# Projecting two value tiles behind the two key tiles of a streaming encoder layer, on one Trainium2 core

## The chip, the core and the metric

The kernel runs on one core of a Trainium2 chip. It is one launch. The metric is the device time of the execution in microseconds (us); lower is better. Engines are named as the profile names them: PE (TensorE matmul), PEld (its weight load), DVE (VectorE), ACT (ScalarE), POOL (GpSimd) and SP (SyncE, which here only issues DMAs).

## The reference, cut to what matters

Two layers, each `x <- x + W_out[silu(gates) * concat(A, B, C, D)]`, for a prompt of 1024 positions and 8 short requests of 16 positions (1152 positions in all). All branch inputs come from one projection of `rmsnorm(x)` (D_MODEL 1024). The change lies in branch A, the RWKV-7 time mixing:

```python
prev = concat([shift_prev, za[:, :-1]])            # token shift
zs = za + rw_mu * (prev - za)
r, k, v, wd, ad = split(zs)                         # 256, 256, 256, 64, 64 wide
decay = exp(-exp(w_log(tanh(wd))));  a = sigmoid(... ad ...)
kk = normalise(k * rw_kk);  k = k * (1 + (a - 1) * rw_ka)
for t in range(T):                                  # per head of 64
    s = s * w_t + (s @ -kk_t) (kk_t * a_t)^T + v_t k_t^T
    y_t = s @ r_t
```

The other branches are latent attention (B), a spatial gating unit (C) and trailing means (D).

## The kernel before, in words

**Layout.** Activations lie with channels on the partitions. A layer's input projection is 24 tiles of 128 output channels (`F_ORDER` gives their order, and with it the order in which weights are loaded). Each tile is made in three groups of 384 positions (g = 0, 1, 2), each group by 24 matmuls of 128x384 into one of two `pj` buffers in PSUM. `project` (L245) loops over groups, then over 8 pieces of the contraction, with three products each, since float32 is split into a high and a low part (`xh`, `xl`, `wh`, `wl`); `load_weights` (L229) makes the parts of a weight, on ACT (L241) and POOL (L242). Nearly all matmuls are issued by one helper, so their line is L76. I write K1g2 for group 2 of tile K1, and so on. After a group its *sink* runs on ACT and DVE.

**The order of branch A.** WDAD (decay and a) and K0 come together, then K1, R0, R1 (receptance), V0, V1 (values), then D0, GD0 (branch D and its gate), D1 and so on:

```python
project([(l, WDAD), (l, K0)], ...)           # K0's sink starts a_elem(0, g)
shifted(K1, ..., after_k1)                   # K1's sink starts a_elem(1, g), then queues systems(g - 1)
go("a", idle(4)); go("a", systems(2)); go("a", idle(4)); go("a", solve())
receptance(0, R0); receptance(1, R1)
values(V0); values(V1)
A.dma_start(out=shift_o[l], in_=sho)
pool_in(0, D0)
go("a", recurrence())
```

**Side work.** `a_elem`, `systems`, `solve` and `recurrence` are generators in a lane "a". While a projection is written out, `tick` takes the next step of the lane, so that its instructions stand between the projection's matmuls. A build step then orders the instructions of every engine once more and allocates the rotating buffers. Each engine runs its own list strictly in its order.

- `a_elem(i, g)` (L427 to L487): decay, `a`, the normalised key and the operands `kb` and `ar` of half i and group g. A chain over ACT and DVE that begins with a square (L437), whose sum over channels is a PE matmul `st<-ea,cr`; DVE reads it at L447 and ends the chain at L487.
- `systems(g)` (L506 to 518): for each of 18 chunks of 64 positions, four small matmuls `b<-ar,kb`, a masked copy to a two-buffer tile `ns` (DVE L514) and a DMA of it to DRAM (`nd`, for the last two `nds`; ACT's queue, L515). The operands come from both halves, so chunk 0 needs K0 and K1 of group 0.
- `solve()` (L520 to 553): loads all chunks' systems back (SP, L528 and L529), inverts them on DVE by column steps, first 16 wide, then 32 wide (31 steps of L538 and L540), copies the result transposed (L550) and writes it to DRAM (`dd`, ACT's queue, L552 and L553, two each).
- `recurrence()` (L707): the chunks in the order 16, 17 (the short requests), 0, 1, ... 15. `prepare(c)` (L560) loads the inverse (`tt`; for chunk 0 on from `dd`, SP, L571) and makes what does not need the state (gm by L580, L590 to L636). `advance(c)` (L639) carries the state (L655, L662, L666 and so on). The recurrence is queued behind D0 in both programs.
- `receptance` (L489) multiplies `ar` on POOL. `values` (L495) only writes the shifted tile `m`, which `prepare` transposes and the group norm reads; nothing of `a_elem`, `systems` or `solve` reads it.
- The shift sink (L381 to 400): ACT L383 and L386, DVE L387 and L390, for group 2 also DVE L395 and L397 and ACT L399 and L400.
- GD0's sink: ACT L756 to L758, DVE L759, the matmul `st<-m,pbd`, DVE L820, a DMA (ACT's queue, L822).

Of the kernel before, what the change touches and what calls it, by code (L numbers as in the profile page):

```python
# [31 lines left out]
(WDAD, K0, R0, V0, K1, R1, V1, D0, GD0, D1, GD1, VC0, VC1, U0, GC0, U1, GC1,  # L32
 GB0, GB1, Q0, Q1K, CK, GA0, GA1) = range(NF)

F_ORDER = (WDAD, K0, K1, R0, R1, V0, V1, D0, GD0, D1, GD1, VC0, VC1, U0, GC0, U1, GC1,
           Q0, Q1K, CK, GB0, GB1, GA0, GA1)


# [10 lines left out]
def tile_trunk(ctx: ExitStack, tc: tile.TileContext, *aps):  # L49
# [37 lines left out]
    def nm(p):  # L87
        cnt[0] += 1
        return f"{p}_{cnt[0]}"
# [20 lines left out]
    def s_tile(tag, bufs, cols=G):  # L110
        return sp_.tile([128, cols], F32, tag=tag, name=nm(tag), bufs=bufs)
# [13 lines left out]
    def go(lane, gen):  # L125
        lanes.setdefault(lane, deque()).append(gen)

    def start(lane, gen):
        next(gen)
        go(lane, gen)  # L130
# [26 lines left out]
    def gcols(g):  # L157
        return slice(g * G, (g + 1) * G)
# [39 lines left out]
    def raw_weights(fi, src):  # L198

        raw[fi] = m_tile(1024).rearrange("p (k t) -> p k t", k=8)  # L200
        SY.dma_start(out=raw[fi], in_=src)
# [3 lines left out]
    SY.dma_start(out=vcs, in_=vec.rearrange("l p n -> p l n"))  # L205
    raw_weights(0, win[0, F_ORDER[0]])
    raw_weights(1, win[0, F_ORDER[1]])
    next(first[1])
# [15 lines left out]
    for l in range(L):  # L224
        plan += [((l, f), win[l, f], range(8)) for f in F_ORDER]
        plan += [((l, NF + f), wout[l, f], out_order) for f in range(8)]
# [118 lines left out]
    for l in range(L):  # L345
# [11 lines left out]
        def vcol(i):  # L357
            return vc[:, i:i + 1]

        def inproj(f, sink):  # L360
            ticks = (3,)
            if f in (K1, R0, R1, V0, V1, D0, GD0, D1, GD1, VC0, VC1, GC0, U1, GC1,
                     GA0, GA1):
                ticks = (2, 5)
            elif f in (U0, GB0, GB1):
                ticks = (1, 3, 5)
            project([(l, f)], xh, xl, [sink], ticks)
# [8 lines left out]
        def shift_sink(f, dest, after=None):  # L376
            last = {}

            def sink(g, ps):
                mu, om = vcol(V_MU + f), nv[:, f:f + 1]  # L380
                zs = dest(g)  # L381
                n = min(G, TP - g * G)
                A.activation(out=zs, in_=ps, func=AF.Copy, scale=om)  # L383
                if n == G:
                    last[g] = smp.tile([128, 1], F32, tag="lc", name=nm("lc"), bufs=4)
                    A.activation(out=last[g], in_=ps[:, G - 1:G], func=AF.Copy)  # L386
                V.scalar_tensor_tensor(out=zs[:, 1:n], in0=ps[:, 0:n - 1], scalar=mu, in1=zs[:, 1:n],  # L387
                                       op0=ALU.mult, op1=ALU.add)
                if g > 0:
                    V.scalar_tensor_tensor(out=zs[:, 0:1], in0=last[g - 1], scalar=mu, in1=zs[:, 0:1],  # L390
                                           op0=ALU.mult, op1=ALU.add)
                if n < G:
                    samp = ps[:, n:].rearrange("p (s t) -> p s t", t=SL)
                    zv = zs[:, n:].rearrange("p (s t) -> p s t", t=SL)
                    V.scalar_tensor_tensor(out=zv[:, :, 1:], in0=samp[:, :, :SL - 1], scalar=mu, in1=zv[:, :, 1:],  # L395
                                           op0=ALU.mult, op1=ALU.add)
                    V.scalar_tensor_tensor(out=zv[:, :, 0], in0=sh0[:, f, :], scalar=mu, in1=zv[:, :, 0],  # L397
                                           op0=ALU.mult, op1=ALU.add)
                    A.activation(out=sho[:, f, 0:1], in_=ps[:, n - 1:n], func=AF.Copy)  # L399
                    A.activation(out=sho[:, f, 1:], in_=samp[:, :, SL - 1], func=AF.Copy)  # L400
                if after:
                    after(g, zs)
            return sink

        def shifted(f, dest, after=None):
            inproj(f, shift_sink(f, dest, after))
# [20 lines left out]
        def a_elem(i, g, k):  # L427
            kb = abp.tile([128, 6, 2, 64], F32, tag="ab", name=nm("kb"))
            ar = abp.tile([128, 6, 2, 64], F32, tag="ab", name=nm("ar"))
            KB[i][g], AR[i][g] = kb, ar  # L430
            gc = gcols(g)

            def ea():
                return s_tile("ea", EA)

            q = ea()
            A.activation(out=q, in_=k, func=AF.Square, scale=vcol(V_KK + i))  # L437
            yield

            pw, pk, pa = st(), st(), pb()  # L440
            mm(pw[:, :G], wlo[0:64, i * 128:(i + 1) * 128], z6[0:64, gc])
            mm(pa[:, :G], wlo[64:128, i * 128:(i + 1) * 128], z6[64:128, gc])
            mm(pk[:, :G], bd1, q)
            rw, av = ea(), ea()
            A.activation(out=rw, in_=pw[:, :G], func=AF.Exp, scale=-1.0, bias=nv[:, 7 + i:8 + i])
            A.activation(out=av, in_=pa[:, :G], func=AF.Exp, scale=-1.0, bias=nv[:, 9 + i:10 + i])
            V.tensor_scalar(out=q, in0=pk[:, :G], scalar1=1e-24, scalar2=None, op0=ALU.max)  # L447
            recip1p(rw)
            cs = ea()
            n = min(G, TP - g * G)  # L450
            V.tensor_tensor_scan(out=cs, data0=smask[:, 0:G] if n == G else smask[:, 128:], data1=rw, initial=0.0,
                                 op0=ALU.mult, op1=ALU.add)
            yield
            A.activation(out=q, in_=q, func=AF.Ln)
            A.activation(out=q, in_=q, func=AF.Exp, scale=-0.5)
            ex = ar[:, :, 1, :]
            A.activation(out=ex, in_=chv(cs), func=AF.Exp, scale=-DECAY_C)
            nch = n // 64
            Po.tensor_copy(out=Pend[:, i, g * 6:g * 6 + nch], in_=ex[:, :nch, 63])
            if n < G:  # L460
                Po.tensor_copy(out=PendS[:, i, :].rearrange("p (c s) -> p c s", c=2),
                               in_=ex[:, nch:].rearrange("p c (s t) -> p c s t", t=SL)[:, :, :, SL - 1])
            V.tensor_tensor(out=rw, in0=cs, in1=rw, op=ALU.subtract)
            ep = rw
            A.activation(out=ep, in_=rw, func=AF.Exp, scale=-DECAY_C)
            ei = cs
            A.activation(out=ei, in_=cs, func=AF.Exp, scale=DECAY_C)
            yield

            kk = q  # L470
            V.scalar_tensor_tensor(out=kk, in0=k, scalar=vcol(V_KK + i), in1=q, op0=ALU.mult, op1=ALU.mult)
            V.scalar_tensor_tensor(out=ar[:, :, 0, :], in0=chv(kk), scalar=-1.0, in1=chv(ep),
                                   op0=ALU.mult, op1=ALU.mult)

            recip1p(av)
            yield
            t = ea()
            V.tensor_tensor(out=t, in0=av, in1=ei, op=ALU.mult)
            for hh in range(2):
                pr = slice(64 * hh, 64 * hh + 64)  # L480
                V.tensor_tensor(out=kb[pr, :, hh, :], in0=chv(kk)[pr], in1=chv(t)[pr], op=ALU.mult)  # L481
            V.tensor_scalar(out=av, in0=av, scalar1=vcol(V_KA + i), scalar2=nv[:, 11 + i:12 + i],
                            op0=ALU.mult, op1=ALU.add)
            V.tensor_tensor(out=av, in0=av, in1=ei, op=ALU.mult)
            for hh in range(2):
                pr = slice(64 * hh, 64 * hh + 64)
                V.tensor_tensor(out=kb[pr, :, 1 - hh, :], in0=chv(k)[pr], in1=chv(av)[pr], op=ALU.mult)  # L487

        def receptance(i, fr):  # L489
            def after(g, zs):  # L490
                ex = AR[i][g][:, :, 1, :]
                Po.tensor_tensor(out=ex, in0=chv(zs), in1=ex, op=ALU.mult)
            shifted(fr, lambda g: s_tile("gn", 3), after)

        def values(fv):  # L495
            v = m_tile()
            shifted(fv, lambda g: v[:, gcols(g)])
            vfm.append(v)
# [406 lines left out]
        def after_k1(g, zs):  # L905
            start("a", a_elem(1, g, zs))
            if g > 0:
# [2 lines left out]
        project([(l, WDAD), (l, K0)], xh, xl,  # L910
                [shift_sink(WDAD, lambda g: z6[:, gcols(g)], tanh_part),
                 shift_sink(K0, lambda g: zk0[:, gcols(g)], lambda g, zs: start("a", a_elem(0, g, zs)))])
        shifted(K1, lambda g: zk1[:, gcols(g)], after_k1)
        go("a", idle(4))
        go("a", systems(2))
        go("a", idle(4))
        go("a", solve())
        receptance(0, R0)
        receptance(1, R1)
        values(V0)  # L920
        values(V1)
        A.dma_start(out=shift_o[l], in_=sho)
        pool_in(0, D0)
        go("a", recurrence())
# [638 lines left out]
```

## Time and profile before

| what | value |
|---|---|
| runs | 1456.58, 1454.72, 1450.95 us (median 1454.72) |
| profiled execution, own time | 1454.34 us |
| its span, first to last instruction | 1452.5 us |
| PE busy | 1373.0 us, 95% |
| DVE, ACT, POOL busy | 54%, 51%, 30% |
| mean granted TensorE clock | 0.987 |

The profile is of one execution. A row of the timeline gives the start in us from the span's start, the duration, engine, line, operation, output and inputs; in brackets the idle time of the engine before it and what ended it. PE's matmuls overlap: a 128x384 row lasts 0.33 us, while in an undisturbed run the next starts after 0.17 us. A float32 matmul of the small kinds is shown as two passes (x8 for a chunk's four).

### The profile page before, as it was taken

Reading aid. Unit: us, or ns where it says so; the run is one execution under the profiler, and the core shown is the slowest. Engines: PE = TensorE matmul, PEld = TensorE weight load, DVE = VectorE, ACT = ScalarE, POOL = GpSimd, SP = SyncE. Lnnn points to the kernel's source line nnn. Section 1 sums busy time; section 2 is a strip of 40 time slices with the busy share of each in tenths; the row PEclk is TensorE's granted clock in tenths of the full one; section 3 lists DMA queues with packets and bytes.
Section 4 is the critical chain, followed back from the end, with each engine's and each line's share of the span. In section 5 each row is a group of like instructions: output and inputs, shape, how many; then the busy total and the mean of one; then the engine's idle time right before and its main releaser. Section 6 shows DMA issues by size and latency. Waiting matters only on the chain. (4 is left out here: it accounts for less than half of the span.)

```text
span 1452.5 us, 26772 instructions
## 1 busy us (share of the span) xinstructions
PE 1373.0 (95%) x9938; PEld 1154.8 (80%) x9938; DVE 783.5 (54%) x1762; ACT 740.7 (51%) x1985; POOL 437.7 (30%) x576
## 2 busy tenths in 40 slices
PE   4899889999999999999989998999999999999999
PEld 3678878888988876679977787788799788666998
DVE  6985944445236557742287858543532474767211
ACT  6772244555366667642257521555643776666210
POOL 4514414336411110322162333332652111112320
PEclk9999999999999999999989999999999999999999
DMA  7213241110312114033301123221022111131232
GB/s 221 52 34 79 56 102 49 56 45 31 103 34 77 53 35 132 3 119 98 88 22 30 50 64 71 85 71 48 31 74 66 58 57 54 44 102 44 70 98 76
DMA packets 116594, 97.38 MB, mean 67 GB/s; under 512 B 46128, under 2 KB 111344, under 8 KB 116464
## 3 DMA queue, kind: packets, MB, share of 16 engines
q1 hardware_dynamic: 76776, 73.74, 17.6%
q10 hardware_dynamic: 39688, 21.94, 5.0%
q8 instruction: 78, 1.28, 0.4%
q14 instruction: 52, 0.43, 0.1%
HBM read 71.48 MB, written 24.16 MB: 66 GB/s over the span
## 5 line engine op out<-in xcount | busy, mean ns | idle before, releaser
L76 PE MATMUL pj<-xh,wh 128*128 128x384 f32 x1152 | 413.8, 360 | 18.0 <-ACT xh L280 7.3
L76 PE MATMUL pj<-xl,wh 128*128 128x384 f32 x1152 | 395.5, 343 | 3.7 <-POOL xl L282 2.7
L76 PE MATMUL pj<-xh,wl 128*128 128x384 f32 x1152 | 395.4, 343 | 0.0
L242 POOL TENSOR_TENSOR wl<-wr,wh 128x256 fp32r<-128x256 f32 x200 | 156.2, 789 | 463.8 <-ACT wh L241 387.5
L76 PEld LDWEIGHTS pj<-xh,wh 128*128 128x128 f32 x1152 | 220.7, 192 | 40.7 <-ACT sho L400 10.0
L76 PEld LDWEIGHTS pj<-xl,wh 128*128 128x128 f32 x1152 | 221.1, 192 | 11.2 <-POOL xl L282 4.7
L76 PEld LDWEIGHTS pj<-xh,wl 128*128 128x128 f32 x1152 | 220.7, 192 | 6.1 <-issue 4.8
L76 PE MATMUL pj<-yh,wh 128*128 128x384 f32 x384 | 130.0, 339 | 2.7 <-DVE x L1386 2.7
L76 PE MATMUL pj<-yh,wl 128*128 128x384 f32 x384 | 129.2, 337 | 0.0
L76 PE MATMUL pj<-yl,wh 128*128 128x384 f32 x384 | 129.0, 336 | 0.0
L241 ACT ACTIVATE wh<-wr 128x256 fp32r<-128x256 f32 x200 | 80.9, 414 | 86.0 <-PE pj L76 41.5
L76 PEld LDWEIGHTS pj<-yh,wh 128*128 128x128 f32 x384 | 72.5, 189 | 4.0 <-DVE x L1386 3.0
L242 POOL TENSOR_TENSOR wl<-m,wh 128x256 fp32r<-128x256 f32 x56 | 43.6, 788 | 103.7 <-ACT wh L241 76.4
L76 PEld LDWEIGHTS pj<-yl,wh 128*128 128x128 f32 x384 | 72.6, 189 | 0.1
L76 PEld LDWEIGHTS pj<-yh,wl 128*128 128x128 f32 x384 | 72.6, 189 | 0.1
L1261 ACT ACTIVATE X<-b,ng 128x512 f32<-128x512 f32 (+3 forms) x96 | 55.0, 576 | 28.7 <-DVE ng L1253 25.0
L76 PEld LDWEIGHTS st<-X,X 128*64 128x64 f32 x576 | 35.5, 136 | 31.6 <-DVE mx L1249 6.3
L76 PE MATMUL b<-sp,cr 128*128 128x384 f32 (+3 forms) x192 | 59.2, 389 | 1.0 <-POOL sp L99 0.6
L1249 DVE TENSOR_REDUCE mx<-b 128x1 f32<-128x512 f32 (+3 forms) x96 | 53.0, 552 | 8.5 <-PE b L76 6.9
L1382 DVE TENSOR_TENSOR pt<-pj,pt 128x384 f32<-128x384 f32 x24 | 13.4, 557 | 80.6 <-PE pj L76 80.6
L241 ACT ACTIVATE wh<-m 128x256 fp32r<-128x256 f32 x56 | 22.5, 413 | 62.2 <-PE pj L76 61.1
L76 PE MATMUL st<-X,X 128*64 128x128 f32 x576 | 53.3, 283 | 0.3
(296 smaller groups left out, 2558.1 us busy)
## 6 DMA issues: line engine op xcount, KB each, us to landing
wr<-in_win_dram SPq DMA_DIRECT2D x176, 128.0 KB
m<-in_wout_dram SPq DMA_DIRECT2D x12, 512.0 KB
x<-in_xT_dram SPq DMA_DIRECT2D x12, 384.0 KB
ysp<-m ACTq DMA_DIRECT2D x24, 192.0 KB
pt<-in_xT_dram SPq DMA_DIRECT2D x24, 192.0 KB
ea<-ysp SPq DMA_DIRECT2D x24, 192.0 KB
x1d<-x ACTq DMA_DIRECT2D x24, 192.0 KB
pt<-x1d SPq DMA_DIRECT2D x24, 192.0 KB
```

What stands on the lines that cost most here:

```text
L76: return PE.matmul(out, lhsT=lhsT, rhs=rhs, start=start, stop=stop, skip_group_check=True)
L241: A.activation(out=h, in_=r, func=AF.Copy)
L242: Po.tensor_tensor(out=lo, in0=r, in1=h.bitcast(F32), op=ALU.subtract)
L1249: V.tensor_reduce(out=mx[:, b:b + 1], in_=pc[:, :w], axis=AX.X, op=ALU.max)
L1261: A.activation(out=P[:, :w], in_=pc[:, :w], func=AF.Exp, scale=SCALE, bias=ng, accum_out=sums[pr][:, b, s, h:h + 1])
L1382: V.tensor_tensor(out=xr, in0=ps, in1=xr, op=ALU.add)
```

## The change

The two calls of `values` move: V0 stands between K0 and K1, V1 in front of R0. `F_ORDER` follows, so the weights are loaded in that order. No operation is added or taken away, and every operand is the same.

```diff
-F_ORDER = (WDAD, K0, K1, R0, R1, V0, V1, D0, GD0, D1, GD1, VC0, VC1, U0, GC0, U1, GC1,
+F_ORDER = (WDAD, K0, V0, K1, V1, R0, R1, D0, GD0, D1, GD1, VC0, VC1, U0, GC0, U1, GC1,
...
+        values(V0)
         shifted(K1, lambda g: zk1[:, gcols(g)], after_k1)
         go("a", idle(4))
         go("a", systems(2))
         go("a", idle(4))
         go("a", solve())
+        values(V1)
         receptance(0, R0)
         receptance(1, R1)
-        values(V0)
-        values(V1)
         A.dma_start(out=shift_o[l], in_=sho)
         pool_in(0, D0)
```

Three places of the first layer show what becomes of the engines' lists; the second layer's are alike.

**PE, where key 1's first sum stands.** `st<-ea,cr` is the sum over channels that `a_elem(1, 0)` waits for. Before, behind five matmuls of K1g2 (here `pj_873`):

```order
L76 MATMUL pj_805<-xh_332,wl_635 128x384
L76 MATMUL b_960<-ar_441,kb_440 64x64 x2
L76 MATMUL pj_873<-xh_405,wh_591 128x384
L76 MATMUL pj_873<-xl_406,wh_591 128x384
L76 MATMUL pj_873<-xh_405,wl_592 128x384
L76 MATMUL pj_873<-xh_405,wh_591 128x384
L76 MATMUL pj_873<-xl_406,wh_591 128x384
L76 MATMUL st_791<-ea_780,cr 128x384
```

Now, behind twelve matmuls of K1g1 (`pj_921`):

```order
L76 MATMUL pj_921<-xh_332,wl_676 128x384
L76 MATMUL pj_921<-xh_332,wh_675 128x384
L76 MATMUL pj_921<-xl_333,wh_675 128x384
L76 MATMUL pj_921<-xh_332,wl_676 128x384
L76 MATMUL st_907<-ea_904,cr 128x384
L76 MATMUL pj_921<-xh_332,wh_695 128x384
```

Counted from K0's end, 53 projection matmuls stood ahead of it (K1g0, K1g1 and five), and now 108 (V0's 72, K1g0 and twelve). K1g2 is followed at once by the first chunks of `systems` in both.

**ACT, at the write of the inverses to `dd`** (`pt_1940` and `pt_2045` are the gates of GD0g0 and GD0g1). Before, it stands ahead of both gates:

```order
L595 ACTIVATE vu_1886<-b_1879 64x2x64 x2
L552 DMA dd_291<-m_1394 64x32x32
L553 DMA dd_291<-m_1393 64x32x32
L552 DMA dd_291<-m_1394 64x32x32
L553 DMA dd_291<-m_1393 64x32x32
L610 ACTIVATE m_1931<-b_1898 128x2x128 x2
L756 ACTIVATE pt_1940<-pj_1856 128x384
```

Now, behind both:

```order
L756 ACTIVATE pt_2045<-pj_1983 128x384
L757 ACTIVATE pt_2045<-pt_2045,eps 128x384
L758 ACTIVATE pt_2045<-pt_2045 128x384
L241 ACTIVATE wh_2090<-wr_2088 128x256
L241 ACTIVATE wh_2120<-wr_2118 128x256
L822 DMA ysp_316<-m_1662 128x384
L241 ACTIVATE wh_2132<-wr_2130 128x256
L241 ACTIVATE wh_2177<-wr_2175 128x256
L552 DMA dd_291<-m_1504 64x32x32
L553 DMA dd_291<-m_1503 64x32x32
```

GD0's first two gates, chunk 16's L610 and the four weight pieces of the group after them no longer queue behind the inverses.

**DVE, inside the 32-wide inversion.** Before, the gates' and chunk 16's operations come after the inversion's copy L550:

```order
L655 TENSOR_TENSOR u_380_1954<-b_1956,u_380_1954 128x128
L580 TENSOR_TENSOR gm_1964<-b_1965,cm 128x256
L759 TENSOR_TENSOR pt_1940<-pj_1856,pt_1940 128x384
L580 TENSOR_TENSOR gm_1964<-b_1969,cm 128x256
L820 SCALAR_TENSOR_TENSOR m_1717<-st_1945,vcs,pt_1940 128x384
L759 TENSOR_TENSOR pt_2045<-pj_1983,pt_2045 128x384
L820 SCALAR_TENSOR_TENSOR m_1717<-st_2050,vcs,pt_2045 128x384
```

Now, they stand between its steps:

```order
L540 TENSOR_TENSOR m_1504<-m_1504,m_1505 128x19x13
L655 TENSOR_TENSOR u_380_1954<-b_1956,u_380_1954 128x128
L538 TENSOR_TENSOR m_1505<-m_1504,m_1503 128x240
L759 TENSOR_TENSOR pt_1940<-pj_1856,pt_1940 128x384
L540 TENSOR_TENSOR m_1504<-m_1504,m_1505 128x20x12
L820 SCALAR_TENSOR_TENSOR m_1662<-st_1945,vcs,pt_1940 128x384
L538 TENSOR_TENSOR m_1505<-m_1504,m_1503 128x231
L580 TENSOR_TENSOR gm_1964<-b_1965,cm 128x256
```

With them an L728 and the two sinks of R1's last groups stand between the inversions' steps now, and the sinks of V0g2 and V1, which stood there, come before them.

In PE's list the tail differs too: from chunk 0's product with `tt` to D1g2's first matmul stood 57 projection matmuls (the last nine of GD0g2, D1g0 and D1g1) and one `st<-m,pbd`; now 21 projection matmuls (of D1g1). From D1g2 on the lists of both programs hold the same operations in the same order: PE's third group of D1 is preceded by the same part of chunk 1.

## Rows read from the trace of the kernel before

**Rows 1.** Windows: start and end, length, then for each engine (PE, PEld, DVE, ACT, POOL) its busy time and, in brackets, its instructions, then the granted TensorE clock as a share of full speed, the busy share of the DMA engines, and GB/s. In order: layer 1 (of two) from K1 to D1g2; the chains of a_elem(1, 0) and (1, 1); the inversions; from chunk 0's product with `tt` to D1g2; an undisturbed stretch of PE; a stretch behind a wait of PE.

```profile
67.70:223.77 156.07, 142.46 (x1100) 123.21 (x1099) 109.10 (x258) 63.34 (x182) 50.01 (x71) 0.98 0.26 66
80.00:100.00 20.00, 17.89 (x106) 12.92 (x104) 19.07 (x38) 15.04 (x38) 4.74 (x8) 1.00 0.08 27
141.17:185.77 44.60, 39.25 (x274) 36.82 (x273) 41.91 (x118) 9.60 (x28) 17.11 (x25) 0.97 0.23 56
201.78:223.77 21.99, 21.75 (x270) 18.50 (x266) 9.19 (x20) 10.55 (x40) 7.29 (x11) 1.00 0.28 88
710.00:720.00 10.00, 10.00 (x59) 10.00 (x58) 2.55 (x5) 1.89 (x4) 2.07 (x3) 1.00 0.33 98
182.60:186.40 3.80, 3.58 (x17) 3.35 (x18) 2.93 (x9) 0.00 (x0) 0.00 (x0) 0.55 0.27 30
```

**Rows 2.** Timeline of PE: the first matmul of K1g2, and key 1's first sum over channels, five matmuls later.

```profile
81.77 0.44 PE L76 MATMUL pj<-xh,wh 128*128 128x384 f32 x1
...
82.76 0.91 PE L76 MATMUL st<-ea,cr 128*128 128x384 f32 x2
```

**Rows 3.** Timeline of DVE: L447 and L487 of a_elem(0, 2) (76.93, 85.79) and of a_elem(1, 0) (83.89, 93.91), then the copies L514 of the first, the third, the tenth and the last chunk, and an L728.

```profile
76.93 0.56 DVE L447 TENSOR_SCALAR ea<-st 128x384 f32<-128x384 f32 x1 [2.61 <-PE st L76]
...
83.89 0.55 DVE L447 TENSOR_SCALAR ea<-st 128x384 f32<-128x384 f32 x1
...
85.79 1.09 DVE L487 TENSOR_TENSOR kb<-m,ea 64x384 f32<-64x384 f32 x2
...
93.91 1.10 DVE L487 TENSOR_TENSOR kb<-m,ea 64x384 f32<-64x384 f32 x2
...
98.00 0.28 DVE L514 TENSOR_TENSOR ns<-b,cm 128x128 f32<-128x128 f32 x1
...
101.87 0.29 DVE L514 TENSOR_TENSOR ns<-b,cm 128x128 f32<-128x128 f32 x1 [0.40 <-DMA nd<-ns]
...
117.61 0.29 DVE L514 TENSOR_TENSOR ns<-b,cm 128x128 f32<-128x128 f32 x1 [0.37 <-DMA nd<-ns]
...
131.69 0.29 DVE L514 TENSOR_TENSOR ns<-b,cm 128x128 f32<-128x128 f32 x1 [1.36 <-DMA nd<-ns]
131.90 1.33 DVE L728 SCALAR_TENSOR_TENSOR gn<-ar,vcs,kb 64x384 f32<-64x384 f32 x2
```

**Rows 4.** Timeline of ACT: the issue of the first two writes of `ns` to DRAM; the first and the last of the four writes to `dd`, and the instruction after them.

```profile
98.48 1.62 ACTq L515 DMA_DIRECT2D nd<-ns  x2
...
184.69 0.66 ACTq L552 DMA_DIRECT2D dd<-m  x1
...
189.25 1.48 ACTq L553 DMA_DIRECT2D dd<-m  x1
190.86 0.66 ACT L610 ACTIVATE m<-b 128x256 f32<-128x256 f32 x2 [14.58 <-issue]
```

**Rows 5.** Timeline of DVE: the copy after the inversions' last step, and what stands behind it (chunk 16, GD0g0's gate, chunk 16's L666).

```profile
184.69 1.08 DVE L550 COPY m<-m 128x1024 f32<-128x1024 f32 x1
192.11 0.29 DVE L655 TENSOR_TENSOR u<-b,u 128x128 f32<-128x128 f32 x1 [6.34 <-ACT u L636]
192.42 0.42 DVE L580 TENSOR_TENSOR gm<-b,cm 128x256 f32<-128x256 f32 x1
193.40 0.56 DVE L759 TENSOR_TENSOR pt<-pj,pt 128x384 f32<-128x384 f32 x1 [0.55 <-ACT pt L758]
...
195.84 2.15 DVE L666 TENSOR_SCALAR m<-vu,mseq_t 128x256 f32<-128x256 f32 x4
```

**Rows 6.** Groups of DVE's instructions by line, from 141.17 to 185.77 us: the sinks of V0g2 and V1. Busy time, mean ns of one, then the idle time before them.

```profile
L387 DVE SCALAR_TENSOR_TENSOR m<-pj,vcs,m 128x255 f32<-128x255 f32 (+1 forms) x4 | 2.2, 539 | 0.0
L390 DVE SCALAR_TENSOR_TENSOR m<-lc,vcs,m 128x1 f32<-128x1 f32 x3 | 1.1, 370 | 0.0
L395 DVE SCALAR_TENSOR_TENSOR m<-pj,vcs,m 128x120 f32<-128x120 f32 x2 | 0.7, 330 | 0.0
L397 DVE SCALAR_TENSOR_TENSOR m<-sh,vcs,m 128x8 f32<-128x8 f32 x2 | 0.4, 220 | 0.0
```

**Rows 7.** Timeline of SP: the load of `tt` for chunk 0, and for the fifth chunk.

```profile
194.41 0.50 SPq L571 DMA_DIRECT2D tt<-dd  x1
...
228.31 0.50 SPq L571 DMA_DIRECT2D tt<-dd  x1
```

**Rows 8.** Timeline of PE: the products with `tt` of chunks 0 and 1, D1g2's first matmul, the product with the fifth `tt`, and D1g2's first matmul in layer 2.

```profile
201.78 0.37 PE L76 MATMUL b<-tt,gm 64*64 64x32 f32 x8
...
210.02 0.37 PE L76 MATMUL b<-tt,gm 64*64 64x32 f32 x8
...
223.77 0.42 PE L76 MATMUL pj<-xh,wh 128*128 128x384 f32 x1
...
234.32 0.42 PE L76 MATMUL b<-tt,gm 64*64 64x32 f32 x8 [0.37 <-DMA tt<-dd]
...
940.44 0.42 PE L76 MATMUL pj<-xh,wh 128*128 128x384 f32 x1
```

**Rows 9.** Timeline of PE: a wait inside GD0g0 and the second and third projection matmul behind it.

```profile
182.54 0.30 PE L76 MATMUL b<-vu,gm 64*64 64x64 f32 x2 [2.94 <-DVE gm L580]
...
184.13 0.52 PE L76 MATMUL pj<-xl,wh 128*128 128x384 f32 x1
184.45 0.52 PE L76 MATMUL pj<-xh,wl 128*128 128x384 f32 x1
```

## The prediction

> **What bounds the kernel now.** I read the windows first, then each engine's timeline around the moved calls. From K1 to D1g2, PE is busy 142.5 of 156.1 us in layer 1, at a mean granted clock of 0.98 [rows 1]: 13.6 us of waiting per layer is all that a new order up to there could win. Past D1g2 both lists are the same, so D1g2's start decides the time. Two other chains run towards it. The first is key 1's on DVE: the sum `st<-ea,cr` at 82.76 [rows 2], L447 at 83.89, L487 from 93.91, the first chunk's copy at 98.00, the last at 131.69 [rows 3]. Then the systems are read back and inverted; the inversions' stretch is 44.6 us with DVE busy 41.9 [rows 1], and its last copy ends at T = 184.69 + 1.08 = 185.77 [rows 5]. The second runs from T: four writes to `dd` on ACT's queue, SP's load of `tt` at 194.41 = T + 8.6 [rows 4, 7], chunk 0's product with it at 201.78 = T + 16.0, D1g2 at 223.77 = T + 38.0 [rows 8]. Layer 2 repeats this: its D1g2 starts at 940.44, 716.7 later [rows 8]. I cost one layer and double it.
>
> **A: key 1's chain starts later.** Between K1g2's first matmul at 81.77 and the sum at 82.76 stand five projection matmuls [rows 2]; now V0g2, K1g0 and half of K1g1 stand there, 60. 59 matmuls take 10.0 us undisturbed, 0.17 each [rows 1], so the 55 more cost 9.4 us: the sum at about 92.1, L447 at 93.3. Not all of it arrives at the copies. Before, DVE was behind: busy 19.1 of 20 us from 80 to 100 [rows 1], it worked off a_elem(0, 2), and from L447 to the first copy took 14.1 us (83.89 to 98.00). The chain of a_elem(0, 2), with less beside it, took 10.0 (76.93 to the end of L487 at 86.88) [rows 3]. The new chain has V0's time to work off key 0, so I give it 10.0, and 1.2 for two operations of a_elem(1, 1) of L447's size that stand between: first copy at 104.5, **+6.5**. From the third copy to the last took 29.8 us for 15, at 1.76 each in the second half (117.61 to 131.69) and more in the first, where the next halves' elements stand between [rows 3]; a copy waits for the DMA of the one two before. The turn is ACT's issue at 98.48 to the third copy at 101.87, 3.4 us [rows 3, 4]. I keep the spacing: last copy +6.5. Bounds: all 15 at 1.76 make 26.4, so +3.1; no backlog saved, +9.4. The read-back behind it (131.69 to 141.17, SP's loads) is unchanged.
>
> **B: other work inside the inversions.** The copy L550 now has chunk 16's L655 (0.29), two L759 (0.56), two L820 (as much) and two L580 (0.42) in front of it [rows 5], together 3.4; an L728 of 1.33 [rows 3], since the receptances on POOL that it follows come later; and two of R1's sinks. Out go the sinks of V0g2 and V1: 2.2 + 1.1 + 0.7 + 0.4 = 4.4 for four, 1.1 each [rows 6]. In 3.4 + 1.3 + 2.2 = 6.9, out 4.4: **+2.5**. Nothing below zero, since no step of the inversion leaves. Twice as much, +5, if the new steps have to wait for ACT or PE in DVE's strict order: the inversion is queued behind each. T moves by 6.5 + 2.5 = 9.0 us; T' is the new T.
>
> **C: what follows T gets shorter.** The gates, chunk 16's L610 and the weight pieces have left the tail of `dd`'s writes on ACT (before, L610 waited there until 190.86) [rows 4]. SP's load goes at T' + 8.6 as before, since the writes are the same. Its landing was not waited for at chunk 0. Nearest rows: 3.4 us for the small `nd` turn above, and 6.0 for the fifth `tt`, issued at 228.31 and released at 234.32 [rows 7, 8]. I take 5.0, nearer to the same transfer: T' + 13.6. The other bound there is PE's: three matmuls of D1g1 stand ahead of the product and need GD0g2's gate, which on DVE is behind chunk 17's four L666. From L610 at T + 5.1 to the end of the L666 at 197.99 took 7.1 us [rows 4, 5]; T' + 5.1 + 7.1 + 0.6 for L759 is T' + 12.8, and the matmuls' end about the same as the landing. I put the product at T' + 14.2, 1.8 earlier than T + 16.0. From it to D1g2 took 22.0, PE busy 21.75 [rows 1], with 57 projection matmuls and one `st<-m,pbd` between; 21 are left. 36 x 0.17 = 6.1, and 0.8 for the other (two passes, as rows 2): 15.1. With so little between them the chunks' small matmuls will wait now and then for DVE and ACT; I add 0.5. D1g2 at T' + 14.2 + 15.6 = T' + 29.8, against T + 38.0: **-8.2**. Bounds: landing after 3.4 and no waits, T' + 27.7 (-10.3); landing after 6.0 and 2.9 us of waits, T' + 32.6 (-5.4).
>
> At no cost: the weights of V0 and V1 come earlier and the receptances' later in SP's queue, in the same pieces; K1 to V1 PE may idle some 2 us for K1g2's chain, and about 7 in front of chunk 16's first L666, which now has to stand behind L550. Both lie under the chain to T', which sets the end there.
>
> **Sum.** 6.5 + 2.5 - 8.2 = +0.8 us a layer, +1.6 for both. The profiled execution took 1454.34 us (span 1452.5), close to the median of 1454.72: 1454.3 + 1.6 = **1455.9**. All bounds at once would be -7.2 and +9.0 a layer.
>
> **A rule on the clock.** Behind a wait of 2.94 us PE's projection matmuls came 0.32 apart (184.13, 184.45), and the granted clock from 182.60 to 186.40 was 0.55, near the lower of its two levels (1.2 of 2.4 GHz) [rows 1, 9]. That is 0.15 us more than undisturbed; for some eight matmuls, about 2.6 us of that window, 1.2 us a wait.
> The Trainium skill, "TensorE: Matmul & The Clock Gate", section "Why this matters for your kernels", tells you to leave no idle gaps of PE between bursts of matmuls, since an idle stretch puts the engine back to half clock; the row agrees. It speaks against this change, which gathers PE's waiting into fewer, longer stretches: by it the time would be the third rival's 1463.1, without it the sum's 1455.9.
>
> **Rivals.**
> *Everything fits (faster).* DVE's backlog is gone by the time key 1's sum comes, the copies run at 1.76 throughout (+3.1), the work inside the inversions fills gaps that DVE has there (44.6 less 41.9 is 2.7 us [rows 1]), +0.5, and C reaches -9.6: -6.0 a layer, 1442.3. For it: DVE was the late one from 80 to 100. Against: the slow half of the copies has the same elements between them.
> *The tail does not shorten (slower).* From one chunk's product with `tt` to the next took 8.2 us (201.78 to 210.02) [rows 8]. If that is the chunk's own chain over PE, ACT and DVE, not the projection beside it, two of them stay, 16.5, and only the last 5.5 us of the 22.0 lose some 1.5: D1g2 at T' + 14.2 + 20.5 = T' + 34.7, C = -3.3, +5.7 a layer, 1465.7. Its place is the stretch between chunk 0's product and D1g2; it decides once D1g2 is later than about T' + 32.7. Against it: PE was busy 21.75 of 22.0 there [rows 1], so before the change projection and chunks filled the time, and no chain showed.
> *The clock.* Up to three long waits a layer, 1.2 us each, outside cover, on top of the sum: +7.2, 1463.1. Against it: most of the waits would have small chunk matmuls behind them, and D1g0's part of the time lies ahead of a wait anyway.
>
> **How the numbers follow.** A measurement of this kernel can tell about 0.5%, 7.3 us, from no change. Chances: the forecast 0.56, everything fits 0.20, the tail 0.17, the clock 0.07. The forecast's own range is 1448 to 1464; of its chance 0.46 lie within 0.5%, 0.04 below, 0.06 above. Everything fits is faster; the tail is slower; the clock's case is split, 0.04 slower and 0.03 the same. Together faster 0.24, same 0.49, slower 0.27. The range reaches from the one rival to the other: 1442 to 1467; the two corners of the bounds beyond it are what is left out.
>
> **What would show it.** In layer 1: key 1's first sum at about 92, the first copy L514 at 104 to 105 and the last near 138; L550's end at 194 to 195, with L655, L759 and L820 among the inversions' steps; SP's load of `tt` 8.6 behind; PE idle about 7 us in front of `b<-m,kbt`; the product with `tt` near 209; D1g2 within 1.5 us of 223.8 + 0.8. A is wrong if the last copy is later by under 4 or over 8 us, B if the inversions take over 50 us, C if D1g2 stands outside T' + 28 to T' + 33. If the lengths agree and the time still differs by over 7 us, then something past D1g2 changed, which I have put at nothing.

## The result: slower by 0.9%, and the profile after

| | before | changed |
|---|---|---|
| runs, us | 1450.95 to 1456.58, median 1454.68 (4) | 1463.35, 1467.09, 1468.63, 1470.99, median 1467.86 |
| ratio, 95% interval | 1 | 1.0093 [1.0072, 1.0115] |
| profiled execution: time, span | 1454.34, 1452.5 us | 1463.35, 1461.6 us |
| mean granted clock | 0.987 | 0.979 (the other three runs 0.974, 0.973, 0.973) |

The changed kernel is 13.2 us slower by the medians, where the forecast was +1.6. One execution of a later kernel (x10) took 2135.93 us at a mean granted clock of 0.559 and is left out of that kernel's figures. The changed kernel's profiled execution is the fastest of the four, +9.0 us. In that execution layer 1 reaches D1g2 8.5 us later than before (232.31 against 223.77 [rows 8]), layer 2 starts 5.0 later, its D1g2 is 10.2 later (950.64 against 940.44), and the span ends 9.1 later. So each layer loses up to D1g2, and some of it comes back behind.

The windows of the changed kernel, with the columns of [rows 1]: the inversions and from T' to D1g2 in layer 1; the same two in layer 2; from the product with `tt` to D1g2; a stretch of PE ahead of T'; and a part of the second stretch.

```profile
148.32:197.79 49.47, 40.36 (x293) 36.96 (x292) 46.91 (x123) 13.95 (x38) 18.20 (x26) 0.93 0.23 60
197.79:232.31 34.52, 30.33 (x306) 24.40 (x306) 12.36 (x29) 10.39 (x41) 5.77 (x10) 0.75 0.37 83
870.51:920.07 49.56, 41.49 (x288) 38.13 (x286) 46.94 (x119) 13.31 (x36) 18.01 (x26) 0.90 0.22 59
920.07:950.64 30.57, 25.73 (x305) 20.97 (x306) 12.46 (x30) 10.38 (x41) 5.77 (x10) 0.89 0.41 94
214.39:232.31 17.92, 16.64 (x227) 13.41 (x226) 7.12 (x15) 6.41 (x29) 5.04 (x9) 0.90 0.26 91
193.00:195.30 2.30, 2.29 (x12) 1.70 (x10) 2.16 (x8) 0.73 (x2) 0.55 (x1) 1.00 0.47 164
198.00:211.00 13.00, 12.02 (x68) 10.11 (x69) 3.27 (x9) 2.42 (x8) 0.11 (x1) 0.50 0.58 91
```

Two things differ from before. DVE is busy 46.9 us in the inversions in place of 41.9, and the stretch is longer by as much. And between T' and D1g2 the granted clock is 0.75 in one layer and 0.89 in the other; from 198 to 211 us it is 0.50, the lower of the two levels (1.2 of 2.4 GHz). Just ahead of T' it is 1.00.

Timeline of DVE in the changed kernel, for [rows 3, 5]: L447 and L487 of a_elem(1, 0), the first and the last copy L514, the first step of the inversions, an L728 between steps, and the copy behind the last step.

```profile
92.12 0.56 DVE L447 TENSOR_SCALAR ea<-st 128x384 f32<-128x384 f32 x1 [1.65 <-PE st L76]
...
101.82 1.09 DVE L487 TENSOR_TENSOR kb<-m,ea 64x384 f32<-64x384 f32 x2
...
104.44 0.28 DVE L514 TENSOR_TENSOR ns<-b,cm 128x128 f32<-128x128 f32 x1
...
139.13 0.29 DVE L514 TENSOR_TENSOR ns<-b,cm 128x128 f32<-128x128 f32 x1 [1.22 <-PE pj L76]
...
148.32 0.16 DVE L538 TENSOR_TENSOR m<-m 32x15 f32<-32x15 f32 x1 [3.27 <-DMA m<-nds]
...
157.96 1.43 DVE L728 SCALAR_TENSOR_TENSOR gn<-ar,vcs,kb 64x384 f32<-64x384 f32 x1
...
196.76 1.03 DVE L550 COPY m<-m 128x1024 f32<-128x1024 f32 x1
```

Timeline of PE in the changed kernel, for [rows 2, 8]: key 1's first sum; chunk 16's first product behind T'; the product with `tt` and D1g2 in layer 1; in layer 2 chunk 16's first product behind T', the product with `tt` and D1g2.

```profile
91.17 0.91 PE L76 MATMUL st<-ea,cr 128*128 128x384 f32 x2
...
198.98 1.97 PE L76 MATMUL b<-m,kbt 128*64 128x256 f32 x8 [3.69 <-DVE m L666]
...
214.39 0.42 PE L76 MATMUL b<-tt,gm 64*64 64x32 f32 x8
...
232.31 0.42 PE L76 MATMUL pj<-xh,wh 128*128 128x384 f32 x1
...
921.27 1.92 PE L76 MATMUL b<-m,kbt 128*64 128x256 f32 x8 [3.03 <-DVE m L666]
...
934.22 0.42 PE L76 MATMUL b<-tt,gm 64*64 64x32 f32 x8 [1.50 <-DMA tt<-dd]
...
950.64 0.42 PE L76 MATMUL pj<-xh,wh 128*128 128x384 f32 x1
```

T' = 196.76 + 1.03 = 197.79, 12.0 later than T. The first load of `tt` on SP's queue, for [rows 7], stands 8.7 behind it (before, 8.6):

```profile
206.48 6.01 SPq L571 DMA_DIRECT2D tt<-dd  x2
```

### The profile page after: what moved, and what is told of

Read it like the earlier page. It is cut to its first block, busy times and chain, and to the rows that moved or that the text cites. A ratio compares the mean times of both kernels' runs of the same rounds, so it can differ in the third digit from the quotient of the medians.

```text
span 1461.6 us, 26763 instructions
## 1 busy us (share of the span) xinstructions
PE 1377.3 (94%) x9938; PEld 1159.8 (79%) x9938; DVE 786.2 (54%) x1762; ACT 741.8 (51%) x1985; POOL 432.8 (30%) x576
## 4 chain that ended last, share of the span: by engine, by line
PE 69%; DVE 17%; DMA 5%; ACT 4%; issue 3%; POOL 2%; ACTq 0%; SPq 0%; DVEq 0%; POOLq 0%
PE pj L76 41%; PE b L76 14%; PE st L76 9%; PE pj L1272 3%; DMA nd<-ns 2%; DVE m L538 2%; DVE ea L278 2%; DVE m L540 2%; DMA tt<-dd 1%; DVE gn L728 1%; DVE m L791 1%; PE b L586 1%; DMA nds<-ns 1%; DMA m<-nds 1%; DVE kb L481 1%
## 5 line engine op out<-in xcount | busy, mean ns | idle before, releaser
L242 POOL TENSOR_TENSOR wl<-wr,wh 128x256 fp32r<-128x256 f32 x200 | 154.8, 781 | 435.9 <-ACT wh L241 399.7
L76 PE MATMUL pj<-yh,wh 128*128 128x384 f32 x384 | 129.3, 337 | 2.4 <-DVE x L1386 2.4
L242 POOL TENSOR_TENSOR wl<-m,wh 128x256 fp32r<-128x256 f32 x56 | 43.5, 788 | 101.5 <-ACT wh L241 74.4
```

The lines of the kernel that those rows point to most:

```text
L76: return PE.matmul(out, lhsT=lhsT, rhs=rhs, start=start, stop=stop, skip_group_check=True)
L242: Po.tensor_tensor(out=lo, in0=r, in1=h.bitcast(F32), op=ALU.subtract)
```

## Experiments

Theory 1: the delay is key 1's, V0 standing in front of K1 (step A). Theory 2: it is the inversions', which now share DVE and POOL with the receptances' work (step B). Theory 3: the tail behind T' does not give back what it should, because PE waits there and its clock falls (step C and the clock rival). The table has, in us, layer 1 / layer 2: from the first matmul of the tile behind K0 to T, the inversions within that, and from T to D1g2; then the granted clock in this last stretch, and the ratio to the kernel before on the same chip.

| kernel | to T | inversions | T to D1g2 | clock there | median; ratio [95%] |
|---|---|---|---|---|---|
| before | 118.1 / 118.8 | 44.6 / 44.5 | 38.0 / 38.2 | .99 / .99 | 1451.1 to 1454.7 |
| changed | 130.7 / 131.7 | 49.5 / 49.6 | 34.5 / 30.6 | .75 / .89 | 1467.86; 1.0093 [1.0072, 1.0115] |
| r_after | 131.7 / 131.5 | 49.4 / 49.5 | 33.5 / 33.3 | .80 / .80 | 1470.05; 1.0134 [1.0116, 1.0153] |
| x1_v0_only | 129.3 / 127.3 | 46.6 / 45.5 | 31.0 / 32.6 | .95 / .84 | 1461.49; 1.0068 [1.0053, 1.0084] |
| x2_v1_only | 121.2 / 120.0 | 47.5 / 48.1 | 37.6 / 38.3 | .93 / .92 | 1455.53; 1.0029 [1.0017, 1.0040] |
| x3_v_behind_k1 | 124.0 / 121.8 | 49.2 / 49.5 | 37.0 / 38.2 | .95 / .92 | 1460.13; 1.0057 [1.0040, 1.0074] |
| x8_product_on_dve | 121.7 / 119.9 | 47.7 / 47.4 | 41.0 / 37.0 | .86 / .99 | 1459.32; 1.0054 [1.0040, 1.0068] |
| x10_before_ns4 | 114.1 / 113.0 | 46.6 / 46.1 | 38.2 / 38.5 | 1.00 / .91 | 1443.51; 0.9937 [0.9924, 0.9950] |
| x11_after_ns4 | 124.8 / 124.2 | 48.6 / 48.4 | 33.9 / 32.1 | .80 / .84 | 1453.60; 1.0008 [0.9998, 1.0018] |

### One part alone: x1, x2, x3

```diff
 # x1_v0_only: V0 before K1, V1 behind the receptances
-F_ORDER = (WDAD, K0, K1, R0, R1, V0, V1, ...
+F_ORDER = (WDAD, K0, V0, K1, R0, R1, V1, ...
 # x2_v1_only: V1 behind K1, V0 behind the receptances
+F_ORDER = (WDAD, K0, K1, V1, R0, R1, V0, ...
 # x3_v_behind_k1: both behind K1, before the receptances
+F_ORDER = (WDAD, K0, K1, V0, V1, R0, R1, ...
```

and the calls `values(...)` moved to match. x2 exchanges the two value halves in the output, since the list of the value tiles is filled in the order of the calls.

> V0 alone stands between K0 and K1; V1 stays behind R1. Theory 1 (key 1's later chain carries the loss): the first copy of a system at about 104.4 and the end of the inversions' copy 8 to 12 us later than before, as with the full change, and the time near it, 1460 to 1469. Theory 2 (the loss comes from the receptances standing later, whose sinks and POOL products then fall into the inversions): they stand one tile later instead of two, so about half of the loss, 1459 to 1462, and the inversions' stretch nearer 47 than 49.5. Theory 3 (PE's clock after the wait in front of chunk 16's product): as theory 1 in the time, with the granted clock near 0.5 behind that wait in at least one layer.

> V1 alone moves, in front of R0; V0 stays behind R1, so key 1's chain is where it was before. Theory 1: first copy at 98, time as before, 1450 to 1458. Theory 2: the receptances stand one tile later, so 4 to 7 us of loss, 1458 to 1462. Theory 3: no long wait of PE in front of chunk 16's product, time as before.

> Both value tiles in front of the receptances, but behind K1: all of the change except the delay of key 1. Theory 1: first copy at 98, time within 4 us of before. Theory 2: the receptances stand two tiles later as in the full change, so its whole loss of 9 to 13 us, 1463 to 1468, with the inversions' stretch at 48 to 50. Theory 3: as theory 1, the granted clock in front of D1g2 as before.

x1, which has A without V1's move, reaches T 11.3 and 8.5 us later than before, of it 2.0 and 1.1 in the inversions. x3 has key 1's chain nearly undelayed (the first copy stands 31.3 us behind the start in layer 1, before 30.3; in layer 2 29.5 in both), and its inversions take 4.6 and 5.0 longer, as in the changed kernel. Theories 1 and 2 both hold, and roughly add up: by the medians +10.3 us for x1 and +9.0 for x3, against +13.2 and, beside these three, +18.9 for the changed kernel. The sum is not exact, since x1 has a part of theory 2 in it, and x3 came out below the 1463 to 1468 expected of theory 2. x2, which has one V behind the receptances and one before them, pays about half of x3 in the time (+4.4). In x3 the tail keeps about its old length, 37.0 and 38.2: T comes 5.9 and 3.0 us later, D1g2 4.9 and 3.0.

### The same kernel again: r_after

> The changed kernel again, for a second profile. Theory 1: every stretch of DVE repeats (first copy 104.4, end of the inversions' copy 197.8), and D1g2 is 5 to 9 us late in either layer. Theory 3: where PE's granted clock stays near 0.5 for another length of time behind the wait in front of chunk 16's product, D1g2 moves with it by up to 4 us in a layer, while DVE's stretches before it don't; runs at a mean granted clock of 0.973 are about 7 us longer than that at 0.979.

The kernel is unchanged, the time another: 1468.76 to 1474.94 us at clocks of 0.969 to 0.972. The time to T agrees with the first profile within 1.0 us; T to D1g2 takes 33.5 and 33.3 at a clock of 0.80 in place of 34.5 at 0.75 and 30.6 at 0.89. The same instructions, so the difference is the clock's. Windows of r_after: both tails.

```profile
201.36:234.90 33.54, 29.35 (x305) 24.00 (x306) 12.35 (x30) 10.37 (x41) 5.77 (x10) 0.80 0.37 86
928.03:961.34 33.31, 29.27 (x306) 23.94 (x306) 12.37 (x30) 10.38 (x41) 5.78 (x10) 0.80 0.37 86
```

What PE did before the clock fell stands in the timelines: in the changed kernel's layer 1 a wait of 3.69 us in front of `b<-m,kbt`, for DVE's L666 behind L550, with the clock at 1.00 until then and at 0.50 from 197.7 for 13.7 us; in its layer 2 a wait of 3.03, and half clock for 3.4 us. In r_after the wait was 2.45 us, and half clock followed for 10.2 us:

```profile
202.56 1.08 PE L76 MATMUL b<-m,kbt 128*64 128x256 f32 x8 [2.45 <-DVE m L666]
```

So the length of the slow stretch does not follow the length of the wait. x1 has the same product behind the same L550, but a shorter wait, since V1's matmuls are still there to run. Its PE row, and its windows from T' on, in layer 1:

```profile
198.93 1.08 PE L76 MATMUL b<-m,kbt 128*64 128x256 f32 x8 [1.70 <-DVE m L666]
```

```profile
197.74:203.00 5.26, 4.07 (x53) 3.28 (x53) 2.85 (x7) 0.00 (x0) 0.00 (x0) 1.00 0.95 156
203.00:208.00 5.00, 4.36 (x32) 3.94 (x31) 0.72 (x3) 2.67 (x11) 0.79 (x2) 1.00 0.56 97
```

In x1's layer 1 the clock stays at 1.00 there, and the product with `tt` comes at T' + 14.6; in the changed kernel at T' + 16.6 in layer 1. In x1's layer 2 the wait is again 1.70 and the clock again 1.00 behind it, but from 929.2 to 939.4 us it is 0.50, beside a wait of 1.88 for the load of `tt`, and the tail takes 32.6 in place of 31.0. A shorter wait at `b<-m,kbt` does not keep the whole tail at full clock.

### The recurrence six slots later: x4 and x9

```diff
+        go("a", idle(6))
         go("a", recurrence())
```

x4 is the changed kernel with this line, x9 the kernel before with it.

> The changed kernel with the recurrence begun six steps later, so that D1g0, D1g1 and the start of D1g2 stand in front of chunk 16's product that needs L666; the order up to the inversions is unchanged (first copy 36.6 us behind K0's end, inversions 49.5). Theory 3 (a part of the loss is PE's clock behind its wait there): no wait of over 2 us and a granted clock of 0.95 or more from T on; 6 to 12 us faster than the changed kernel, 1456 to 1464. Theory 1 and 2 alone (the late T sets the end, whatever PE does meanwhile): as the changed kernel, 1466 to 1472.

> The kernel before with the recurrence begun six steps later: projections of GD0, D1 in place of PE's waits in front of the recurrence (some 8.8 us a layer from the start of the inversions to D1g2). Theory 3: those waits and the low clock behind them go, 1443 to 1448. Without it: the recurrence is the longer chain, the projections run out earlier at its end, and the time is as before or up to 6 us longer.

x4: 1463.21 us, 1.0082 [1.0069, 1.0096]; x9: 1453.00, 1.0008 [0.9999, 1.0018]. In x4 the long wait at T' is gone and the clock is 1.00 for the first 9 us behind it. But the chunks' own waits then come a little later, with nothing to fill them: PE waits 2.55 us for ACT's L802, from 207.4 to 221.1 us the clock is 0.50, and the product with `tt` moves to T' + 19.2. Five to seven us came back, in a run whose mean clock was 0.975 (the changed kernel's: 0.969 to 0.979). So moving the wait does not remove it, and x4 doesn't prove theory 3 by itself.

x9 did not do what it was made for. Its waits did not go but came together in one, 7.13 us in layer 1 and 7.37 in layer 2, of the projection for DVE's L759, which follows L550 in DVE's list and waits for ACT:

```profile
191.10 0.69 PE L76 MATMUL pj<-xh,wh 128*128 128x384 f32 x1 [7.13 <-DVE pt L759]
```

The clock is 0.50 there from 186.5 to 196.7 us, and still the time is that of the kernel before. A slow stretch alone, then, does not tell the time; it counts where the matmuls in it are on the path.

### The writes of `dd` on SP's queue: x7

```diff
-                A.dma_start(out=diagonal(dd, i, 32, 128), in_=DT[64 * i:64 * i + 64])
+                SY.dma_start(out=diagonal(dd, i, 32, 128), in_=DT[64 * i:64 * i + 64])
```

(and the second write likewise), in the kernel before.

> The kernel before with the four writes of the inverses on SP's queue in place of ACT's. If the writes' place on ACT holds up the tail (L610 waited until 190.86 there): the operations of chunk 16 behind the inversions' copy 4 to 5 us earlier, D1g2 2 to 4 us earlier in each layer, 1443 to 1448. If the round trip through DRAM is what counts: D1g2 within 1 us of before, 1449 to 1453.

1455.17 us, 1.0019 [1.0010, 1.0029]: slightly slower. T is 187.52 here. The issue of the four writes on SP ended at T + 6.6 (on ACT, T + 5.0), SP reached its load of `tt` at 201.04, T + 13.5 in place of T + 8.6, and the product with `tt` waited 2.76 us for it, at T + 18.9. The writes are no quicker on the other queue. The load comes 5 us later there because SP's list has a weight load (L238) between the writes and it: this waited 6.4 us for POOL, whose weight split L242 ran from 199.73, and went at 200.48. In the kernel before SP's load waits for the writes themselves. So x7 does not show what the writes' place on ACT costs.

### The receptances' product on DVE: x8

```diff
 # x3, and:
-                Po.tensor_tensor(out=ex, in0=chv(zs), in1=ex, op=ALU.mult)
+                V.tensor_tensor(out=ex, in0=chv(zs), in1=ex, op=ALU.mult)
```

> Both value tiles behind K1 and in front of the receptances, and the receptances' product with the operand on DVE in place of POOL. Theory 2 in the form that POOL's products slow the inversion's steps beside them: the 92 steps take 33.5 to 34.5 us in place of 36.4 and 37.3, although DVE has four products of about 0.55 more to do in the same stretch. If it is only DVE's queue: steps as long as without the move, stretch 2 us longer. Time 1455 to 1462.

Groups of DVE's instructions by line in the inversions (busy time, mean ns; then the idle time before them). Before, with the four groups of the inversions' 92 steps:

```profile
L538 DVE TENSOR_TENSOR m<-m,m 128x31 f32<-128x31 f32 (+15 forms) x31 | 13.4, 433 | 0.8
L540 DVE TENSOR_TENSOR m<-m,m 128x31 f32<-128x31 f32 (+15 forms) x31 | 13.1, 422 | 0.8
...
L538 DVE TENSOR_TENSOR m<-m 32x15 f32<-32x15 f32 (+7 forms) x15 | 3.8, 251 | 1.0 <-DMA m<-nds 0.6
L540 DVE TENSOR_TENSOR m<-m 32x15 f32<-32x15 f32 (+7 forms) x15 | 3.3, 222 | 0.4
```

The changed kernel:

```profile
L540 DVE TENSOR_TENSOR m<-m,m 128x31 f32<-128x31 f32 (+15 forms) x31 | 13.9, 450 | 0.9
L538 DVE TENSOR_TENSOR m<-m,m 128x31 f32<-128x31 f32 (+15 forms) x31 | 13.7, 443 | 0.8
L538 DVE TENSOR_TENSOR m<-m 32x15 f32<-32x15 f32 (+7 forms) x15 | 4.4, 296 | 3.6 <-DMA m<-nds 3.3
...
L540 DVE TENSOR_TENSOR m<-m 32x15 f32<-32x15 f32 (+7 forms) x15 | 3.8, 256 | 0.4
L728 DVE SCALAR_TENSOR_TENSOR gn<-ar,vcs,kb 64x384 f32<-64x384 f32 x2 | 2.0, 1012 | 0.0
L580 DVE TENSOR_TENSOR gm<-b,cm 128x256 f32<-128x256 f32 x4 | 1.7, 417 | 0.0
L820 DVE SCALAR_TENSOR_TENSOR m<-st,vcs,pt 128x384 f32<-128x384 f32 x2 | 1.2, 608 | 0.0
L759 DVE TENSOR_TENSOR pt<-pj,pt 128x384 f32<-128x384 f32 x2 | 1.1, 548 | 0.0
L387 DVE SCALAR_TENSOR_TENSOR gn<-pj,vcs,gn 128x383 f32<-128x383 f32 (+1 forms) x2 | 1.1, 531 | 0.0
```

x8:

```profile
L538 DVE TENSOR_TENSOR m<-m,m 128x31 f32<-128x31 f32 (+15 forms) x31 | 14.0, 452 | 0.7
L540 DVE TENSOR_TENSOR m<-m,m 128x31 f32<-128x31 f32 (+15 forms) x31 | 12.4, 401 | 0.7
...
L540 DVE TENSOR_TENSOR m<-m 32x15 f32<-32x15 f32 (+7 forms) x15 | 3.8, 250 | 0.4
L538 DVE TENSOR_TENSOR m<-m 32x15 f32<-32x15 f32 (+7 forms) x15 | 3.4, 226 | 0.4
L492 DVE TENSOR_TENSOR ar<-gn,ar 128x384 f32<-128x384 f32 x5 | 3.3, 657 | 0.1
```

The same 92 steps take 33.6 us before, 35.8 in the changed kernel, 36.4 in x3 (its groups: 14.6, 13.5, 4.7, 3.6) and 33.6 in x8: with the receptances' products away from POOL the steps are as quick as before. DVE pays 3.3 us for five products, and the inversions still end 1.5 to 2.1 us sooner than in x3. The time did not follow: 1459.32 against 1460.13, with overlapping intervals. In the profiled execution layer 1's tail took 41.0 at a clock of 0.86, layer 2's 37.0 at 0.99, with the same instructions.

How POOL holds up DVE can be read step by step. The changed kernel's DVE, and its POOL in the same stretch:

```profile
150.77 1.01 DVE L538 TENSOR_TENSOR m<-m 32x55 f32<-32x55 f32 x1
151.81 0.66 DVE L540 TENSOR_TENSOR m<-m 32x55 f32<-32x55 f32 x1
152.51 0.67 DVE L538 TENSOR_TENSOR m<-m 32x60 f32<-32x60 f32 x1
153.21 0.72 DVE L540 TENSOR_TENSOR m<-m 32x60 f32<-32x60 f32 x1
153.96 0.21 DVE L538 TENSOR_TENSOR m<-m 32x63 f32<-32x63 f32 x1
```

```profile
150.70 1.01 POOL L492 TENSOR_TENSOR ar<-gn,ar 128x384 f32<-128x384 f32 x1 [0.27 <-DVE gn L390]
151.67 2.19 POOL L242 TENSOR_TENSOR wl<-wr,wh 128x256 fp32r<-128x256 f32 x3
```

POOL's product ends at 151.71, and the step beside it at 151.78. The three weight splits L242 end at 152.41, 153.11 and 153.86; the next steps end at 152.47, 153.18 and 153.93. Each step ends 0.07 us behind one POOL instruction, and once POOL is idle a larger one takes 0.21. Before, a step of 32x55 took 0.20:

```profile
143.76 0.20 DVE L538 TENSOR_TENSOR m<-m 32x55 f32<-32x55 f32 x1
```

The Trainium skill, "SBUF — State Buffer", section "Who interferes with whom", says that a DVE instruction with two SBUF inputs contends with a GpSimd instruction that reads SBUF, over a port pair that one holds for its whole instruction while the other is blocked. The trace agrees, in these four steps to 0.07 us.

### Four buffers for the copies: x10 and x11

```diff
-                ns = chp.tile([128, 2, 64], F32, tag="u0", name=nm("ns"), bufs=2)
+                if c % 4 < 2:
+                    ns = chp.tile([128, 2, 64], F32, tag="u0", name=nm("ns"), bufs=2)
+                else:
+                    ns = chp.tile([128, 4, 64], F32, tag="vu", name=nm("ns"), bufs=2)[:, 0:2, :]
```

x10 is the kernel before with this edit, x11 the changed one. A copy then waits for the DMA of the one four before it, not two. (Behind this edit line numbers are three higher.)

> The kernel before with four buffers in turn for a chunk's masked system in place of two, so that a copy waits for the DMA of the one four before. If the DMA's turn sets the copies' pace: first to last copy 28 to 30 us in place of 33.7 and 35.1, the end of the inversions' copy 4 to 6 us earlier in each layer, D1g2 1 to 3 us earlier (PE has 8.8 us of waits there to give), 1445 to 1450. If PE or DVE sets the pace: stretch and time as before, 1450 to 1454.

> The changed kernel with the same four buffers. If the lateness of the inversions' end is what costs: it comes 3 to 6 us earlier against K0's end (129.9 and 131.7 us in the changed kernel), and the time falls by 4 to 10 us, to 1459 to 1466. If the number and place of PE's waits and the clock behind them count alone: same waits, 1466 to 1472.

x10: 1443.51 us, 0.9937 [0.9924, 0.9950] against the kernel before. It is the fastest kernel here, ahead of both. Its windows: first to last copy, and T to D1g2.

```profile
97.99:124.43 26.44, 26.07 (x220) 22.11 (x221) 19.07 (x45) 10.29 (x27) 8.54 (x10) 1.00 0.21 62
181.88:220.05 38.17, 34.64 (x395) 29.33 (x393) 16.76 (x37) 17.06 (x60) 8.80 (x14) 1.00 0.41 99
```

The copies take 26.4 us in place of 33.7. T comes at 181.88, 3.9 earlier than before; the tail is as long as before, and D1g2 is 3.7 earlier. Of the 7.3 us at the copies, 1.4 goes back at the read-back and 2.0 in the inversions, whose 92 steps take 35.6 us there in place of 33.6, though no more of POOL's large instructions stand beside them than before. x11 gains as much on the changed kernel and more: 1453.60, 1.0008 [0.9998, 1.0018], level with the kernel before and below the expected range. (The 129.9 in its expectation is counted from 0.8 us behind the first matmul of the tile; from that matmul it is 130.7.) The pair shows that the chain to T sets the time in both orders: in x10 T comes 3.9 us earlier in layer 1 and, from the start of that layer's stretch, 5.8 in layer 2, and the time fell by 9.3 by the medians.

## Why the prediction was wrong

**What bounds the kernel** was right. The chain to T and the chain behind it set D1g2, and x10 moved T by 3.9 us in layer 1 and D1g2 by 3.7.

**A, key 1's delay, +6.5: right in kind, small by one.** The sum stood at 91.17 (forecast about 92.1), L447 at 92.12, L487's end at 102.91, so the chain took 10.8 us where I gave it 10.0. The first copy came at 104.44, +6.4 (forecast 104.5), the last at 139.13, +7.4, the first step +7.2. In layer 2 the delay up to the first step was 7.8. The copies' spacing, which I kept, grew by 1.0 in layer 1.

**B, the inversions, +2.5: this step failed, at half of what it was.** Measured +4.9 and +5.1, at the upper bound. The count of what comes and goes was right but for one size: the two L728 took 2.0 in place of 1.33, so +3.1 net (in 7.5 by the groups above and the smaller ones of the sinks and L655, L580 counted by the two more than before; out 4.4 [rows 6]). What I missed is the other 2.2: the steps themselves grew from 33.6 to 35.8, beside POOL. Together that is 5.3 us of DVE's time in a stretch that became 4.9 longer. I had written "Nothing below zero, since no step of the inversion leaves", and did not ask whether a step would stay as short. x8 has the products off POOL and the steps back at 33.6. They are not the only thing that counts, though: x10's steps took 35.6 beside no such product, so which step falls beside which POOL instruction may count as much; no run tests that alone.

**C, the tail, -8.2: this step failed too.** Measured -3.5 in layer 1 and -7.6 in layer 2; in r_after -4.5 and -4.9. In layer 2 it came almost as worked out: the product with `tt` at T' + 14.15 (forecast 14.2), D1g2 at T' + 30.6 (29.8). In layer 1 the same list gave T' + 16.6 and T' + 34.5. What lies between is the clock: 0.89 against 0.75 over the stretch, 25.7 against 30.3 us of busy PE for the same matmuls. I had seen PE's idle time in front of `b<-m,kbt` coming (about 7 us; it was 3.69 and 3.03), and put it under "at no cost", since it lay under the chain to T'. The wait itself was. But the 13.7 us at half clock behind it were on the path. (The upper bound for C also has a slip: with the 0.6 us from landing to product that the forecast has, it is T' + 33.2, not 32.6. Layer 1 and both layers of r_after, 33.5 and 33.3, lie beyond that too.)

Per layer the sum was 6.5 + 2.5 - 8.2 = +0.8; layer 1 measured 7.2 + 4.9 - 3.5 = +8.5, layer 2 7.8 + 5.1 - 7.6 = +5.3. Over both layers A was 2.0 us too small, B 5.0 and C 5.3, so B's miss weighs as much as C's. "Past D1g2 both lists are the same", priced at nothing, was 3.5 us off in layer 1 (+8.5 at D1g2, +5.0 at layer 2's start) and 1.1 in layer 2, both in the kernel's favour. That goes with the clock of the execution and not with the order: from D1g2 to layer 2's start took 518.3 us at a clock of 0.990 before, 514.7 at 0.997 in this execution, and 518.7 at 0.987 in r_after.

**The rivals.** "Everything fits" is out. "The tail does not shorten" named T' + 34.7, which layer 1 happens to show, but not its mechanism: from the product to D1g2 took 17.9 and 16.4 in place of its 20.5. "The clock" had the mechanism; its price was wrong. I charged 1.2 us a wait, from eight slow matmuls in one row of before; one wait here was followed by 13.7 us at half clock, and PE's busy time behind T' grew by 4.6 us from one layer to the other. The rule of the Trainium skill that stands beside it ("TensorE: Matmul & The Clock Gate", "Why this matters for your kernels"), no idle gaps of PE between bursts of matmuls, agrees with these rows in its direction.

**The rest of the 13.2 us** is that same clock, run by run. The profiled execution, +9.0, had 0.979; the others had 0.973 and 0.974. Over 132 timed runs, each taken against the mean of its own kernel, a run is 0.69 us longer for each 0.001 of mean clock that it has less. Eight runs of the changed kernel average 1469.2 us at 0.9726, 55 of the kernel before 1452.0 at 0.9871: 14.5 x 0.69 = 10.0 of the 17.2 us go with the clock, some 7 with the rest. That is a correlation. What is shown is the same list in two layers and two executions with different clocks and lengths, and in x8's two layers. That the wait in front of `b<-m,kbt` is what lowers the clock is not shown: with it shorter (x1) or gone (x4) the clock fell at other places of the tail. A kernel that keeps PE busy through the waits with nothing else changed was not tried, so how much a full clock would give back stays open.

## What to carry to other kernels

Before you move work ahead of a serial chain, add up what the chain gains in length, on every engine that it shares a port with: here 12 to 13 us at T a layer, for a tail that gave back 3.5 to 7.6. A wait of PE that lies under another chain is not free when the matmuls behind it are on the path; price it by the stretch at low clock, and allow for that to vary between executions. And look at the chain's slowest turn first: two more buffers for the copies gave 0.6%, while every other order of the value tiles tried here lost.

## What the runs showed of the hardware that I had not expected

- A DVE step of 32x55 elements took 1.01 us beside a POOL product, and 0.20 without one.
- One program's eight runs lay between 1463.35 and 1474.94 us with mean clocks from 0.979 to 0.969; the kernel before stayed between 1448.0 and 1456.6. Within one series of runs the spread was alike (7.6 and 6.2 us against 5.6 to 7.6), so it is not shown that an order with long PE waits is the less steady one.
